# Sample rows: readouts gathered behind the fifth chunk step, new states computed beside the second feed-forward block

## The chip, the cores and the metric

The kernel runs on one core of a Trainium2 chip. A core has five engines with queues of their own: TensorE (PE, matmuls; its weight loads are shown as PEld), VectorE (DVE), ScalarE (ACT), GpSimd (POOL) and SyncE (SP, which here issues DMAs). Each works through its own queue in order, and an instruction whose input is not there holds all that stand behind it on that engine. The metric is the device time of one execution in microseconds (us); lower is better.

## The reference

One inference step of a small hybrid decoder: a half-step SwiGLU feed-forward block, a mixer, a second half-step feed-forward block and a final RMS norm. It works on one prompt of 512 tokens and on 8 sample rows, each a single new token with a stored state. The mixer has a pooling part and a state-space part with 16 heads of 64, in two groups, and a state of 128 per head and channel. For the prompt the state-space part is evaluated in chunks of 128 tokens. For a sample row it is one step of the recurrence:

```python
dt = softplus(dt_raw + dt_bias);  A = -exp(a_log)
h_new = exp(dt * A) * h0 + (dt * x) outer B      # 64 x 128 for each head
y     = h_new @ C  +  d_skip * x
y     = rms_norm_by_group(y * silu(z)) * ssd_norm
```

`y` goes on through the output projection, and `h_new` (8 rows, 16 heads, 64 x 128, 4 MB in float32) is an output itself. The feed-forward blocks compute `h + 0.5 * (silu(x @ wg) * (x @ wu)) @ wd` with 2816 hidden columns.

## The kernel before, in words

Tokens lie along the free dimension: 520 columns, 512 of the prompt and 8 samples, worked in two halves of 260. Every float32 product is made of three matmuls (`mm3`, lines 115 to 118) on a high and a low part; `split` (line 101) makes the parts of a weight tile with a cast on ACT (line 106) and a subtraction on DVE (line 107).

The feed-forward block (`Ffn`) goes through 22 tiles of 128 hidden columns. `step(f)` (line 329) runs one tile: seven products (`product`, line 264) on 7 combinations in place of 8, each evacuated by ACT (line 284); `gates` (silu on ACT, line 292) and `close` (cast of the hidden tile g on ACT, line 299, and its low part on DVE, line 300). `load` (line 245) fetches the tile's weights into one of two raw pairs by SP and splits them. After 8, 8 and 6 tiles, `down` (line 339), and for the last chunk `down_by_half`, multiplies the chunk by the down weights and adds it to `h`. The factor -0.5 times each token's norm factor is a tile `rn`, made once by `scales` (line 302) and applied at lines 356 and 408.

The mixer follows lists written by hand: CONV_PLAN, then GATE_PLAN, then LAST_PLAN. A letter and a number name a stage: `b`, `x` convolution tiles; `p`, `c`, `m` pooling; `A`, `B` the two halves of a chunk step (`ssd_a`, `ssd_b`; number j is chunk j % 4 of group j // 4); `z` gate projection; `sN` the next N sample items; `G`, `H` gate and norm of a group; `o`, `g`, `h` the output projection's three parts; `n` the first tile of the second feed-forward block. A sample item is a pair (row b, group g), 16 in all, group 0 first. The lists give the order in which instructions are traced; a scheduler, which simulates the program, then orders each engine's queue: traced earlier is preferred, but what is ready may pass. `keep_in_program_order` pins an instruction behind the one traced before it on its engine, and `issue_after` behind a named one; neither adds a wait for a result.

A sample item (`sample`, line 760) loads B and C of its row, broadcast to 128 partitions (`bcb`, line 764), and the state `h0` (256 KB, line 767) by SP; for each of four quarters ACT makes dt x B (line 771) and DVE the new state (line 772); SP stores the state (line 774); and DVE forms the readout, a product with C summed along the row (line 776). `gate` (line 877) multiplies with silu(z), and `gate_out` (line 888) squares, norms and splits for the output projection. The tiles `h0`, `bcb` and `ho` have two buffers each.

Of the kernel before, what the change touches and what calls it, by code (L numbers as in the profile page):

```python
# [9 lines left out]
F32 = mybir.dt.float32  # L10
# [6 lines left out]
P = 128  # L17
# [44 lines left out]
def tile_trunk_step(ctx: ExitStack, tc: tile.TileContext, ins: dict, outs: dict):  # L62
# [132 lines left out]
    class Ffn:  # L195
# [4 lines left out]
        def __init__(self, nx, i, wx, gp, direct):  # L200
            self.nx, self.i, self.wx, self.gp, self.direct = nx, i, wx, gp, direct
            self.w, self.A, self.BE, self.ac, self.g, self.tg, self.raw, self.banks, self.behind = ({} for _ in range(9))

# [98 lines left out]
        def scales(self):  # L302
            rstds(self.nx, f"f{self.i}")
            self.rn = self.wx.tile([P, NT], F32, tag="rn", bufs=1, name=f"rn{self.i}")
            nc.vector.tensor_scalar(out=self.rn, in0=self.nx[3], scalar1=-0.5, scalar2=None, op0=ALU.mult)

# [71 lines left out]
        def down_by_half(self, c, lo, after, wd):  # L378
# [26 lines left out]
            def done(d, b):  # L405
                hs = HALVES[b]
                t = self.wx.tile([P, 2, HB], F32, tag="tg", bufs=2, name=f"th{self.i}_{d}{b}")[:, 0]
                nc.vector.tensor_tensor(out=t, in0=banks[d, b][:, :HB], in1=self.rn[:, hs], op=ALU.mult)
                nc.vector.tensor_tensor(out=h[:, d, hs], in0=t, in1=h[:, d, hs], op=ALU.add)
                after(d, b, hs)  # L410
# [127 lines left out]
    f2["ffn"].rest(before2, after2)  # L538
    for p in (ps[0], g2, f2["hg"], f2["wx"]):
        p.release()  # L540


def mixer(tc, ins, outs, e):
    nc = tc.nc
    cst, act, wp, tmp, dr, pool = (e[x] for x in ("cst", "act", "wp", "tmp", "dr", "pool"))
    bank, load_unit, mm3, ws, v, rstd, rstds, vec, h, nx2, raw_tile, open_f2, fin, fill = (
        e[x] for x in ("bank", "load_unit", "mm3", "ws", "v", "rstd", "rstds", "vec", "h", "nx2", "raw_tile",
# [56 lines left out]
    rstds(nx2[0], "mx")  # L604
    dv = mp.tile([48, NT], F32, tag="h0", bufs=2, name="dv")
    for b, hs in enumerate(HALVES):
# [84 lines left out]
    def pooling(g):  # L691
# [15 lines left out]
        nc.gpsimd.tensor_tensor(out=cur[:, first], in0=cur[:, first], in1=rcnt[:, : w - 1], op=ALU.mult)  # L707
        held["pool"] = nc.gpsimd.tensor_tensor(out=cur[:, first], in0=cur[:, first], in1=U[:, first], op=ALU.subtract)
        nc.gpsimd.tensor_copy(npp[:, g], U[:, SEQ : SEQ + PAST])
# [22 lines left out]
    sdt = mp.tile([P, NX, NS], F32, tag="sdt", name="sdt")  # L732
    sdec = mp.tile([P, NX, NS], F32, tag="sdec", name="sdec")
    sxdt = mp.tile([P, NX, NS], F32, tag="sxdt", name="sxdt")
    ysm = mp.tile([P, NX, NS], F32, tag="ysm", name="ysm")
    scr_bc = dr.tile([NS, 512], F32, name="scr_bc")

    def sample_decay():
# [9 lines left out]
    def sample_bc():  # L748
        bcs = bank("bcs")
        for j in range(4):  # L750
            nc.tensor.transpose(bcs[:NS, j * P : (j + 1) * P], BC[:, j, SEQ:NT], ident)
        bct = mp.tile([NS, 512], F32, tag="ho", bufs=2, name="bct")
        nc.scalar.copy(bct, bcs[:NS, :])
        nc.sync.dma_start(out=scr_bc, in_=bct)

    def sample_x(g):
        gs = slice(4 * g, 4 * g + 4)
        nc.vector.tensor_tensor(out=sxdt[:, gs], in0=sdt[:, gs], in1=X[:, gs, SEQ:NT], op=ALU.mult)

    def sample(b, g):  # L760
        gs = slice(4 * g, 4 * g + 4)
        shp = [P, 4, P]
        bcb = mp.tile([P, 2, P], F32, tag="bcb", bufs=2, name=f"bcb{b}{g}")
        nc.sync.dma_start(out=bcb, in_=scr_bc.rearrange("b (a g n) -> b g a n", a=2, g=2)[b, g].unsqueeze(0)
                          .to_broadcast([P, 2, P]))
        h0 = mp.tile(shp, F32, tag="h0", bufs=2, name=f"h0_{b}{g}")
        nc.sync.dma_start(out=h0, in_=ins["state_ssm"][:, b, gs])
        o = mp.tile(shp, F32, tag="ho", bufs=2, name=f"ho_{b}{g}")
        for q in range(4):
            j = 4 * g + q  # L770
            nc.scalar.activation(out=o[:, q], in_=bcb[:, 0], func=AF.Copy, scale=sxdt[:, j, b : b + 1])
            nc.vector.scalar_tensor_tensor(out=h0[:, q], in0=h0[:, q], scalar=sdec[:, j, b : b + 1], in1=o[:, q],
                                           op0=ALU.mult, op1=ALU.add)
        nc.sync.dma_start(out=outs["nss"][:, b, gs], in_=h0)
        for q in range(4):
            nc.vector.scalar_tensor_tensor(out=o[:, q], in0=h0[:, q], scalar=1.0, in1=bcb[:, 1], op0=ALU.mult,
                                           op1=ALU.mult, accum_out=ysm[:, 4 * g + q, b : b + 1])

# [109 lines left out]
    def gate_out(g):  # L888
        zs = zbox[0]
        ry = mp.tile([P, NT], F32, tag="wph", name=f"yr{g}")  # L890
        acc = act.tile([P, NT], F32, tag="acc", name=f"yacc{g}")
        for b, hs in enumerate(HALVES):
            sq = [acc[:, hs]] + [tmp.tile([P, HB], F32, tag="ta", name=f"ysq{g}{q}{b}") for q in range(1, 4)]
            for q in range(4):
# [13 lines left out]
    def samples(n):  # L908
        for _ in range(n):
            if smp:  # L910
                with tc.issue_after(held["pool"].ins):
                    sample(*smp.pop(0))

# [133 lines left out]
```

## Time and profile before

| | us |
|---|---|
| median of 3 runs | 1028.15 |
| lowest, highest | 1027.37, 1032.51 |
| the profiled execution: time | 1030.91 |
| the profiled execution: span, first to last instruction | 1029.1 |

In the profile the first feed-forward block lies roughly between 0 and 370 us, the mixer up to 665 us, the second block from there to the end, with its last tile's output after 985 us. Busy time is the time in which an engine has at least one instruction running, taken from the trace; for PE, whose matmuls are pipelined, a stretch without gaps still says nothing of the rate, which the granted clock and the number of matmuls show. A row of a timeline gives start, length, engine, line, operation, output and inputs by the program's names, shape and count, and in brackets the idle time before it with what ended it. A row of waits reads "who waits, at which line, for whom", with the total, the number of times and the longest.

### The profile page before, as it was taken

Reading aid. Unit: us, or ns where it says so; the run is one execution under the profiler, and the core shown is the slowest. Engines: PE = TensorE matmul, PEld = TensorE weight load, DVE = VectorE, ACT = ScalarE, POOL = GpSimd, SP = SyncE. Lnnn points to the kernel's source line nnn. Section 1 sums busy time; section 2 is a strip of 40 time slices with the busy share of each in tenths; the row PEclk is TensorE's granted clock in tenths of the full one; section 3 lists DMA queues with packets and bytes.
Section 4 is the critical chain, followed back from the end, with each engine's and each line's share of the span. In section 5 each row is a group of like instructions: output and inputs, shape, how many; then the busy total and the mean of one; then the engine's idle time right before and its main releaser. Section 6 shows DMA issues by size and latency. Waiting matters only on the chain.

```text
span 1029.1 us, 19313 instructions
## 1 busy us (share of the span) xinstructions
PE 981.7 (95%) x7848; PEld 956.6 (93%) x7848; DVE 807.3 (78%) x1403; ACT 526.4 (51%) x884; POOL 57.0 (6%) x109
## 2 busy tenths in 40 slices
PE   7999999999999999997698999999999999999994
PEld 6999999999999999996598999899999999999994
DVE  7999557995578788689989877999954799557866
ACT  7566314663145555775486525656631566315552
POOL 0000000000000000337201000000000000000000
PEclk9999999999999999999899999999999999999997
DMA  5333223232232143355354222222323323232203
GB/s 186 111 124 123 83 87 119 83 124 82 88 118 93 55 138 116 126 173 183 110 174 145 94 103 82 69 96 91 115 83 103 103 88 119 82 103 104 93 32 83
DMA packets 45352, 110.25 MB, mean 107 GB/s; under 512 B 5896, under 2 KB 17096, under 8 KB 45264
## 3 DMA queue, kind: packets, MB, share of 16 engines
q1 hardware_dynamic: 45264, 109.03, 31.4%
q8 instruction: 61, 1.00, 0.4%
q14 instruction: 27, 0.22, 0.1%
HBM read 101.67 MB, written 7.34 MB: 106 GB/s over the span
## 4 chain that ended last, share of the span: by engine, by line
PE 42%; DVE 7%; ACT 4%; DMA 2%; issue 1%; POOL 1%; DVEq 0%; ACTq 0%; SPq 0%
PE A L116 4%; PE A L117 4%; PE A L118 4%; PE dn L118 3%; PE dn L116 3%; PE dn L117 3%; PE BE L116 3%; PE BE L118 3%; PE BE L117 3%; PE wo L116 2%; PE wo L118 2%; PE wo L117 2%; PE P L228 1%; PE dh L116 1%; DMA bcb<-scr_bc 1%
## 5 line engine op out<-in xcount | busy, mean ns | idle before, releaser
L356 DVE TENSOR_TENSOR td<-dn,rn 128x520 f32<-128x520 f32 x40 | 27.9, 699 | 112.5 <-PE dn L118 112.5
L116 PE MATMUL dn<-g,whi_1d 128*128 128x260 f32 x352 | 99.3, 283 | 1.7 <-ACT whi_1d L106 1.5
L117 PE MATMUL dn<-g,whi_1d 128*128 128x260 f32 x352 | 99.2, 282 | 0.0
L118 PE MATMUL dn<-g,wlo_1d 128*128 128x260 f32 x352 | 99.1, 283 | 0.0
L116 PE MATMUL dn<-g,whi_2d 128*128 128x260 f32 x256 | 72.5, 283 | 1.6 <-ACT whi_2d L106 1.6
L117 PE MATMUL dn<-g,whi_2d 128*128 128x260 f32 x256 | 72.3, 282 | 0.0
L118 PE MATMUL dn<-g,wlo_2d 128*128 128x260 f32 x256 | 72.1, 283 | 0.0
L116 PEld LDWEIGHTS dn<-g,whi_1d 128*128 128x128 f32 x352 | 66.1, 188 | 2.4 <-ACT whi_1d L106 2.0
L284 ACT COPY ac<-A 128x260 f32<-128x260 f32 x123 | 46.0, 375 | 41.3 <-PE A L118 39.7
L117 PEld LDWEIGHTS dn<-g,whi_1d 128*128 128x128 f32 x352 | 66.2, 188 | 0.0
L118 PEld LDWEIGHTS dn<-g,wlo_1d 128*128 128x128 f32 x352 | 66.1, 188 | 0.0
L106 ACT CAST whi_1d<-raw_1d 128x1024 fp32r<-128x1024 f32 (+1 forms) x24 | 23.4, 980 | 70.6 <-PE dn L117 62.2
L228 PE MATMUL P<-xg_f,raw 128*128 128x260 f32 x192 | 46.2, 398 | 5.3 <-DMA raw<-in_w1gu 5.2
L106 ACT CAST whi_2d<-raw_2d 128x1024 fp32r<-128x1024 f32 (+1 forms) x18 | 18.5, 1027 | 63.6 <-PE dn L117 59.2
L116 PEld LDWEIGHTS dn<-g,whi_2d 128*128 128x128 f32 x256 | 48.3, 189 | 2.0 <-ACT whi_2d L106 2.0
L256 DVE TENSOR_TENSOR s<-raw 128x1024 f32<-128x1024 f32 x41 | 49.9, 1217 | 0.0
L117 PEld LDWEIGHTS dn<-g,whi_2d 128*128 128x128 f32 x256 | 48.2, 188 | 0.0
L228 PEld LDWEIGHTS P<-xg_f,raw 128*128 128x128 f32 x192 | 37.5, 199 | 11.5 <-ACT xg_f L178 5.2
L118 PEld LDWEIGHTS dn<-g,wlo_2d 128*128 128x128 f32 x256 | 48.1, 188 | 0.0
L116 PE MATMUL wo<-catg,whi_wo 128*128 128x260 f32 x128 | 37.4, 292 | 0.2 <-DVE h L871 0.2
L116 PE MATMUL inz<-xh_mx,whi_inz 128*128 128x260 f32 x128 | 37.4, 292 | 0.0
L118 PE MATMUL inz<-xh_mx,wlo_inz 128*128 128x260 f32 x128 | 36.9, 288 | 0.0
(1334 smaller groups left out, 3920.3 us busy)
## 6 DMA issues: line engine op xcount, KB each, us to landing
raw<-in_w2gu SPq DMA_DIRECT2D x44, 512.0 KB, 3.7
raw<-in_w1gu SPq DMA_DIRECT2D x42, 512.0 KB, 4.4
raw_1d<-in_w1d SPq DMA_DIRECT2D x16, 512.0 KB, 3.7
raw_2d<-in_w2d SPq DMA_DIRECT2D x16, 512.0 KB, 4.4
raw_wo<-in_w_out SPq DMA_DIRECT2D x12, 512.0 KB, 4.6
h<-in_state_ssm SPq DMA_DIRECT2D x16, 256.0 KB, 4.8
ab<-scr_acs SPq DMA_DIRECT2D x8, 512.0 KB, 5.2
out_nss<-h SPq DMA_DIRECT2D x16, 256.0 KB, 3.3
```

The source lines that it names most:

```text
L106: nc.scalar.copy(h, src)
L116: nc.tensor.matmul(ps, whi, xhi, start=start, stop=False, **kw)
L117: nc.tensor.matmul(ps, whi, xlo, start=False, stop=False, **kw)
L118: nc.tensor.matmul(ps, wlo, xhi, start=False, stop=stop, **kw)
L228: nc.tensor.matmul(self.banks[f, u][b][:, :HB], ws(self.raw[f][:, u], j + 4 * q), xg[:, slot[q]], start=j == q == 0, stop=j == 3 and q == ...
L256: nc.vector.tensor_tensor(out=s1, in0=diag, in1=up0, op=ALU.add)
L284: nc.scalar.copy(keep, out[:, :HB])
L356: nc.vector.tensor_tensor(out=t, in0=banks[d][:, :, :HB], in1=self.rn.rearrange("p (b t) -> p b t", b=2), op=ALU.mult)
```

## The change

- **Readouts.** With C.h_new = exp(dt A) (C.h0) + (C.B) dt x, the readout no longer needs the new state. `sample` loads C alone (`cb`, in the tag `ta`, three buffers) and `h0` (now four buffers) and forms C.h0, four DVE operations for each item, each pinned. `sample_bc` adds the products C.B for all rows (one DVE operation, one matmul with ones, one ACT copy), and `sample_y`, three small DVE operations at the start of `gate`, puts the parts together.
- **New states.** A generator, `new_states`, called once in each `step(f)` of the second feed-forward block with f > 2: the first call loads B's row and `h0` of the first item; each of the next 16 loads the following item and processes one with eight ACT copies of 128 x 128 with a scale (dt x B, and exp(dt A) h0), an accumulating DMA that adds the one to the other in SBUF, and the store, both DMAs issued by POOL. Loads and copies are pinned. The states are so loaded twice.
- **Order.** GATE_PLAN has its first `s` after B4 and z3, group 0's eight items ahead of G0, which goes from before z4 to behind z5, and group 1's eight between B6 and G1, which goes from before o2 to behind it. `sample`'s `issue_after` goes.
- **Scale and squares.** `rn` goes; lines 356 and 408 multiply by -0.5 and by the norm in one operation. `gate_out` squares four full rows into X in place of eight half rows into `acc` and `ta`.

```diff
 GATE_PLAN = (
-    "s2 A4 z0 B3 z1 s2 m3 z2 s2 B4 z3 s2 A5 G0 z4 B5 A6 z5 s2 s2 z6 s2 A7 z7 B6 s2 o0 H0 o1 B7 G1 o2 "
+    "A4 z0 B3 z1 m3 z2 B4 z3 s2 A5 z4 s2 B5 A6 z5 s2 s2 G0 z6 A7 z7 B6 s2 o0 H0 s2 o1 B7 s2 o2 s2 G1 "
     "o3 g0 g1 H1 g2 g3"
 )
...
         def scales(self):
             rstds(self.nx, f"f{self.i}")
-            self.rn = self.wx.tile([P, NT], F32, tag="rn", bufs=1, name=f"rn{self.i}")
-            nc.vector.tensor_scalar(out=self.rn, in0=self.nx[3], scalar1=-0.5, scalar2=None, op0=ALU.mult)
...
         def step(self, f):
+            if self.states is not None and f > 2:
+                next(self.states, None)
...
-                nc.vector.tensor_tensor(out=t, in0=banks[d][:, :, :HB], in1=self.rn.rearrange("p (b t) -> p b t", b=2),
-                                        op=ALU.mult)
+                nc.vector.scalar_tensor_tensor(out=t, in0=banks[d][:, :, :HB], scalar=-0.5,
+                                               in1=self.nx[3].rearrange("p (b t) -> p b t", b=2), op0=ALU.mult,
+                                               op1=ALU.mult)
...
     g2 = f2["ffn"].gp = pool("g2", "left")
+    f2["st"] = pool("st2", "left")
+    f2["ffn"].states = f2["states"](f2["st"])
...
+        dots = bank("dots")[:, : 2 * NS]
+        nc.vector.tensor_tensor(out=sbc, in0=BC[:, 0:2, SEQ:NT], in1=BC[:, 2:4, SEQ:NT], op=ALU.mult)
+        nc.tensor.matmul(dots, ones, sbc.rearrange("p g b -> p (g b)"), start=True, stop=True)
+        nc.scalar.copy(sbc, dots.rearrange("p (g b) -> p g b", g=2))
...
     def sample(b, g):
+        cb = tmp.tile([P, HB], F32, tag="ta", name=f"cb{b}{g}")[:, :P]
+        nc.sync.dma_start(out=cb, in_=rows_bc(b, 1, g))
+        h0 = mp.tile([P, 4, P], F32, tag="h0", bufs=4, name=f"h0_{b}{g}")
+        nc.sync.dma_start(out=h0, in_=ins["state_ssm"][:, b, 4 * g : 4 * g + 4])
+        for q in range(4):
+            tc.keep_in_program_order(
+                nc.vector.scalar_tensor_tensor(out=junk, in0=h0[:, q], scalar=1.0, in1=cb, op0=ALU.mult, op1=ALU.mult,
+                                               accum_out=ysm[:, 4 * g + q, b : b + 1]))
+
+    def sample_y(g):
         gs = slice(4 * g, 4 * g + 4)
...
+        xb = mp.tile([P, 4, NS], F32, tag="xb", name=f"xb{g}")
+        nc.vector.tensor_tensor(out=xb, in0=sxdt[:, gs], in1=sbc[:, g : g + 1].to_broadcast([P, 4, NS]), op=ALU.mult)
+        nc.vector.tensor_tensor(out=ysm[:, gs], in0=ysm[:, gs], in1=sdec[:, gs], op=ALU.mult)
+        nc.vector.tensor_tensor(out=ysm[:, gs], in0=ysm[:, gs], in1=xb, op=ALU.add)
+
+    def new_states(wx):
+        def load(b, g):
+            br = wx.tile([P, P], F32, tag="sb", bufs=2, name=f"br{b}{g}")
+            tc.keep_in_program_order(nc.sync.dma_start(out=br, in_=rows_bc(b, 0, g)))
+            hs = wx.tile([P, 4, P], F32, tag="sh", bufs=2, name=f"hs{b}{g}")
+            tc.keep_in_program_order(nc.sync.dma_start(out=hs, in_=ins["state_ssm"][:, b, 4 * g : 4 * g + 4]))
+            return br, hs
+
+        todo = [(b, g) for g in range(2) for b in range(NS)]
+        ahead = load(*todo[0])
+        for i, (b, g) in enumerate(todo):
+            yield
+            br, hs = ahead
+            if i + 1 < len(todo):
+                ahead = load(*todo[i + 1])
+            o = wx.tile([P, 4, P], F32, tag="so", bufs=2, name=f"so{b}{g}")
+            for q in range(4):
+                j = 4 * g + q
+                for t, u, s in ((o, br, sxdt), (hs, hs[:, q], sdec)):
+                    tc.keep_in_program_order(
+                        nc.scalar.activation(out=t[:, q], in_=u, func=AF.Copy, scale=s[:, j, b : b + 1]))
+            nc.gpsimd.dma_start(out=hs, in_=o, accum_op=ALU.add)
+            nc.gpsimd.dma_start(out=outs["nss"][:, b, 4 * g : 4 * g + 4], in_=hs)
...
     def gate(g):
         zs = zbox[0]
         gs = slice(4 * g, 4 * g + 4)
+        sample_y(g)
...
-            sq = [acc[:, hs]] + [tmp.tile([P, HB], F32, tag="ta", name=f"ysq{g}{q}{b}") for q in range(1, 4)]
-            for q in range(4):
-                nc.scalar.activation(out=sq[q], in_=zs[:, 4 * g + q, hs], func=AF.Square)
-            rstd(ry, sq, hs, 512, f"y{g}{b}")
+            rstd(ry, [X[:, 4 * g + q, hs] for q in range(4)], hs, 512, f"y{g}{b}")
```

More of the change, by code (lines that the diff above doesn't have):

```diff
@@ L538, in tile_trunk_step @@
     f2["ffn"].rest(before2, after2)
-    for p in (ps[0], g2, f2["hg"], f2["wx"]):
+    for p in (ps[0], f2["st"], g2, f2["hg"], f2["wx"]):
         p.release()
@@ L732, in mixer, with rows_bc @@
     sdt = mp.tile([P, NX, NS], F32, tag="sdt", name="sdt")
-    sdec = mp.tile([P, NX, NS], F32, tag="sdec", name="sdec")
-    sxdt = mp.tile([P, NX, NS], F32, tag="sxdt", name="sxdt")
+    sdec = cst.tile([P, NX, NS], F32, tag="sdec", name="sdec")
+    sxdt = cst.tile([P, NX, NS], F32, tag="sxdt", name="sxdt")
     ysm = mp.tile([P, NX, NS], F32, tag="ysm", name="ysm")
+    sbc = mp.tile([P, 2, NS], F32, tag="sbc", name="sbc")
+    junk = act.tile([P, NT], F32, tag="acc", name="junk")[:, :P]
     scr_bc = dr.tile([NS, 512], F32, name="scr_bc")
+    def rows_bc(b, a, g):
+        return scr_bc.rearrange("b (a g n) -> b a g n", a=2, g=2)[b, a, g].unsqueeze(0).to_broadcast([P, P])
     def sample_decay():
@@ L769, in sample @@
-        for q in range(4):
[L770 to L777, printed above, removed]
+        cb = tmp.tile([P, HB], F32, tag="ta", name=f"cb{b}{g}")[:, :P]
@@ L910, in samples @@
             if smp:
-                with tc.issue_after(held["pool"].ins):
-                    sample(*smp.pop(0))
+                sample(*smp.pop(0))
     pooled, box = [], {}
```

23 lines of the change are left out of this document (10 added, 13 removed).

## The prediction

> **What bounds the kernel now.** I read the page's head, then the busy time by stage, then who TensorE (PE) waits for.
>
> ```profile
> span 1029.1 us, 19313 instructions
> PE 981.7 (95%) x7848; PEld 956.6 (93%) x7848; DVE 807.3 (78%) x1403; ACT 526.4 (51%) x884; POOL 57.0 (6%) x109
> ```
>
> PE is busy for 981.7 of 1029.1 us. Whatever removes work from another engine can return at most the 47.4 us in which PE idles, plus what slow clocks cost. The second view cuts the mixer's second half into stretches; its columns are the busy time (and instructions) of PE, weight loads, DVE, ACT and POOL, then the granted clock, the DMA share and GB/s.
>
> ```profile
> 440.00:500.00 60.00, 47.18 (x371) 42.01 (x369) 56.60 (x154) 36.01 (x87) 33.13 (x47) 0.94 0.49 158
> 500.00:560.00 60.00, 53.08 (x420) 49.82 (x421) 54.21 (x172) 40.89 (x88) 7.58 (x9) 0.94 0.46 148
> 560.00:575.00 15.00, 15.00 (x129) 14.07 (x128) 15.00 (x53) 9.37 (x17) 2.22 (x2) 1.00 0.44 149
> 575.00:632.00 57.00, 56.80 (x447) 54.61 (x446) 44.97 (x75) 21.76 (x34) 1.24 (x1) 1.00 0.24 84
> ```
>
> From 440 to 560 us PE idles 12.8 + 6.9 = 19.7 us while DVE is busy for 110.8 of 120 us. From 575 us on, in the output projection, PE is full again and DVE has 12.0 us to spare. The waits of PE between 400 and 640 us (total, times, longest) say on whom:
>
> ```profile
> PE yd L837 <- DVE ab L822: 7.7, 3, 3.5
> PE pst L834 <- DVE E L848: 6.8, 1, 6.8
> PE px L794 <- ACT X L673: 1.4, 1, 1.4
> PE pst L834 <- POOL xw L821: 1.2, 1, 1.2
> ```
>
> The two long ones, 14.5 us, end on DVE. Both belong to the chunk steps (ssd_a, ssd_b), whose DVE instructions stand in one queue with everything else. After the longest gap PE also runs slowly:
>
> ```profile
> 490.00:495.00 5.00, 1.18 (x2) 0.50 (x2) 5.00 (x11) 1.28 (x4) 1.68 (x5) 0.62 0.31 93
> 495.00:500.00 5.00, 3.82 (x23) 2.26 (x21) 5.00 (x15) 2.19 (x4) 1.29 (x2) 0.70 0.34 120
> 500.00:505.00 5.00, 4.33 (x23) 4.33 (x24) 5.00 (x20) 3.99 (x8) 0.35 (x2) 0.66 0.22 65
> ```
>
> PE's busy 1.18, 3.82 and 4.33 us at granted clocks of 0.62, 0.70 and 0.66 lose 0.4 + 1.1 + 1.5 = 3.0 us against a full clock. So 22.7 us can be won here and no more.
>
> **Mixer: what leaves DVE.** The sample rows' work on DVE is L772 (new state) and L776 (readout). Busy time of L772 in the first and the second 60 us, then the same for L776 (whose count includes one accumulator read for each readout):
>
> ```profile
> 440.00:500.00 60.00, 9.66 (x28) 0.94 0.49 158
> 500.00:560.00 60.00, 8.22 (x28) 0.94 0.46 148
> ```
>
> ```profile
> 440.00:500.00 60.00, 9.97 (x52) 0.94 0.49 158
> 500.00:560.00 60.00, 6.43 (x52) 0.94 0.46 148
> ```
>
> So each stretch holds 28 new-state operations and 26 readouts. What one holds the queue for I take from start to start, since successive instructions overlap:
>
> ```profile
> 447.20 1.66 DVE L772 SCALAR_TENSOR_TENSOR h<-h,sdec,ho 128x128 f32<-128x128 f32 x6
> ...
> 448.77 0.28 DVE L776 SCALAR_TENSOR_TENSOR ho<-h,bcb 128x128 f32<-128x128 f32 x1
> ...
> 448.98 0.29 DVE L776 SCALAR_TENSOR_TENSOR ho<-h,bcb 128x128 f32<-128x128 f32 x1
> ```
>
> Six of L772 in 1.66 us, counted as 1.57 us to the next row at 448.77, are 0.26 us each; a readout with its accumulator read is 0.21 us. The change takes all L772 out of the mixer and puts every readout behind the fifth chunk step. The first stretch loses 28 x 0.26 + 26 x 0.21 = 12.8 us of DVE time. The second loses the same 12.8 us and receives the eight rows of group 0, 32 readouts, 6.7 us, and four of the seven small new operations (the other three go to the later gate or to the earlier transposes), at most a readout's 0.21 us each, 0.8 us: a relief of 5.3 us. The rows of group 1 now stand between the output projection's units, another 32 x 0.21 = 6.7 us, and lie in the 12.0 us that DVE has free there; without that cover they would delay the gate of group 1 by 6.7 us at most. Together DVE is relieved by 18.1 us where PE waits for it.
>
> Not all of that reaches PE: about a quarter of PE's 19.7 us of waiting (19.7 - 14.5 = 5.2) ends on others or in short steps. I take three quarters of 18.1: **-13.6 us**. The ends are 0 (the chain of the chunk steps waits for something else next) and -22.7 us (all idle and all slow clock gone). What also leaves here and is priced at nothing: 64 ACT copies, 16 stores of 256 KB and the wait of the SP queue before each, since they only compete with the same steps and their gain is inside the same 22.7 us. The added matmul with ones and its copy, and the sums of squares done as four full rows in place of eight halves, lie under PE's 56.80 busy us of 57 or among those chunk steps.
>
> What the pin adds on DVE: a readout that waits for its broadcast row or its state (three and four buffers ahead) holds everything behind it, the chunk steps' ab, E and hst among it, and PE waits for those. Its bounds are 0 and the whole gain of the second stretch, 5.3 us.
>
> **Second feed-forward block: what arrives.** Sixteen steps (f = 4 to 19) each get eight ACT copies of 128x128, two loads on SP's queue and two DMAs on POOL's. The same form on ACT, eight in a row:
>
> ```profile
> 525.77 2.45 ACT L771 ACTIVATE ho<-bcb,sxdt 128x128 f32<-128x128 f32 x8
> ```
>
> A set costs 2.45 us. Two steps of the block, columns as before:
>
> ```profile
> 702.35:712.45 10.10, 10.10 (x87) 10.10 (x86) 9.97 (x14) 6.25 (x11) 0.00 (x0) 1.00 0.29 104
> 712.45:722.55 10.10, 10.10 (x87) 10.10 (x86) 9.37 (x13) 6.45 (x11) 0.00 (x0) 1.00 0.30 106
> ```
>
> PE has no gap in 10.10 us; ACT goes from 6.4 to 8.9 us, which fits. But DVE is busy for 9.4 to 10.0, so 0.1 to 0.7 us a step is all that it can lose. The copies are pinned behind the silu of the step before (L292). ACT and DVE there:
>
> ```profile
> 711.26 0.64 ACT L292 ACTIVATE tg<-tg 128x520 f32<-128x520 f32 x1
> 712.26 1.05 ACT L106 CAST whi_6a<-raw 128x1024 fp32r<-128x1024 f32 x1 [0.36 <-PE A L117]
> 713.31 0.63 ACT L299 CAST g<-tg 128x520 fp32r<-128x520 f32 x1
> 714.06 0.38 ACT L284 COPY ac<-A 128x260 f32<-128x260 f32 x1
> 715.13 1.06 ACT L106 CAST shi_6c<-s 128x1024 fp32r<-128x1024 f32 x1 [0.69 <-PE BE L117]
> ```
>
> ```profile
> 713.74 1.22 DVE L107 TENSOR_TENSOR wlo_6a<-raw,whi_6a 128x1024 fp32r<-128x1024 f32 x1
> 714.87 0.69 DVE L300 TENSOR_TENSOR g<-tg,g 128x520 fp32r<-128x520 f32 x1
> 716.22 1.23 DVE L107 TENSOR_TENSOR slo_6c<-s,shi_6c 128x1024 fp32r<-128x1024 f32 x1 [0.65 <-ACT shi_6c L106]
> ```
>
> If the eight run as one block from 711.9 to 714.35, the cast of g, the copy ac and the cast whi_6a queue behind it, and DVE, free at 713.74, waits about 1.2 us for g's cast (714.35 + 0.63) and again for whi_6a. Yet g is read only by the down product, and whi_6a by a product of the next step, so DVE can take other work of the block first, and ACT's own gaps (0.36, 0.69 and later ones) absorb the block within the step. The ends are 0 and 2.45 x 16 = 39 us; I take 0.15 us a step, near the lower end because both engines' sums stay under 10.10: **+2.4 us**.
>
> The transfers. Landing times (min, median, max) of the state load and of the state store in the mixer, and the weight loads on SP's queue in this block:
>
> ```profile
> DMA to landing us min/median/max: 3.3/4.8/7.4
> ```
>
> ```profile
> DMA to landing us min/median/max: 2.0/3.3/5.4
> ```
>
> ```profile
> 708.58 0.33 SPq L249 DMA_DIRECT2D raw<-in_w2gu  x1
> ...
> 718.68 0.33 SPq L249 DMA_DIRECT2D raw<-in_w2gu  x1
> ```
>
> With two buffers, a state's slot must pass copies, accumulating DMA, store and next load within two steps, 20.2 us: 2.45 + 3.3 + 4.8 = 10.6 leave 9.6 us for the accumulating DMA. The trace of before has none. Nearest rows: one load, 4.8 us, below; the slowest load and store in series, 12.8 us, above. I take 4.8, since it too is one transfer of 256 KB into SBUF. Then nothing waits. SP issues the weights of a step 10 us early (708.58 for a cast at 722), so a load pinned ahead of them may wait some 5 us unseen. POOL's queue is otherwise empty (0.00 us). The page "SBUF — State Buffer" of the Trainium skill (the "DVE blocks DMA" trap) speaks against this part: a DMA issued from POOL has its descriptors written by POOL's cores, which certain DVE instructions lock out. No run here shows such a DMA; the Trainium skill's "DMA: Bandwidth & Descriptors" (anatomy of one DMA) would give 2.0 us plus 0.6 us for 256 KB, an estimate by which the sum stays as it is.
>
> **The folded -0.5.** The operation at L305 goes, and the 56 multiplications after it gain a scalar:
>
> ```profile
> L305 DVE TENSOR_SCALAR rn<-r_f x2: 418/420/421, 29.7 to 671.4; 128x520 f32<-128x520 f32 x2
> ```
>
> ```profile
> L286 DVE TENSOR_TENSOR ac<-ac 128x260 f32<-128x260 f32 x41 | 17.2, 421 | 0.4 <-ACT ac L284 0.4
> ...
> L187 DVE SCALAR_TENSOR_TENSOR xd_f<-xd_f,xg_f 128x260 f32<-128x260 f32 x8 | 3.4, 420 | 0.0
> ```
>
> Two operands with or without a constant take the same, so 2 x 0.4 us go and nothing comes: **-0.8 us** at most; I take -0.8.
>
> **Sum.** -13.6 + 2.4 - 0.8 = -12.0 us. The profiled execution took 1030.91 us (span 1029.1), 2.8 above the median of the runs, 1028.15; from the first it gives 1018.9, from the median **1016**, which I forecast.
>
> **The rivals.**
> - *Everything in the mixer comes back*: all 22.7 us, 1028.15 - 22.7 - 0.8 + 2.4 = 1007. For it: DVE is full in the stretch with the gaps. Against: 5.2 us of the waits are not DVE's. Chance 0.10.
> - *Another wait takes the place*: the chunk steps' own order, or pinned readouts that wait for their rows, leave 5 us of the gain: 1028.15 - 5 - 0.8 + 2.4 = 1025. For it: ACT and POOL also end waits. Chance 0.14.
> - *Slower, in the feed-forward block*: ACT's block of copies holds the casts, DVE loses the 2.45 us less its spare 0.7, 1.75 us x 16 = 28 us: 1028.15 - 13.6 - 0.8 + 28 = 1042. It decides from 14.4 / 16 = 0.9 us a step. For it: DVE's 9.4 to 10.0 of 10.10. Against: what is delayed first is needed late. Chance 0.16.
> - *The accumulating DMA is slow*: at 12.8 us the slot's round is 23.4 us, 11.7 a step, 1.6 more x 13 steps (the first of each chunk has the down product to catch up) = 21 us: 1028.15 - 14.4 + 21 = 1035. Chance 0.08. The trap that the Trainium skill names would act here; nothing in the trace bears it out.
> - *It does not do what it says*, the copies fall elsewhere than into these steps: the pins leave ACT no other place, so it has no chance of its own.
>
> **Numbers.** The forecast has 0.52. Under 1023 (0.5%, about what can be told from no change) lie it, the first rival and 0.06 of the second: 0.68. Within 0.5% lie the rest of the second and 0.03 of the third, growing by little: 0.11. Slower: 0.21. The range from 1004 to 1036 leaves out the third rival's upper part; the likeliest case's own is 1010 to 1022.
>
> **What would show it.** L822 and L848 no longer end PE's waits near 470 and 490 us, and the clock stays at 1.00; about 28 readouts fewer before z3; in steps f = 4 to 19 PE stays at 10.10 us with ACT near 8.9. I am wrong if these steps grow, if copies wait on the state's load, or if PE's idle time from 440 to 560 us stays near 20 us.

## The result, and the profile after

The changed kernel takes 1020.51 us (median of 5 runs, 1018.54 to 1022.85), against 1028.15 before (the same median, now of 5 runs, 1027.37 to 1032.51). The ratio on record is 0.9909, with a 95% interval of 0.9895 to 0.9924: faster by 0.9%, or 9.4 us. The quotient of the two medians is 0.9926, a gain of 7.6 us, so the gain is 0.7 to 0.9%. The profiled execution took 1020.51 us, with a span of 1018.5 us at a mean granted clock of 0.991; before, the span was 1029.1. Those spans, which the traces below explain, differ by 10.6 us: the profiled execution of before lay 2.8 us above its median.

The head of the page of the changed kernel (busy time, share of the span, instructions):

```profile
span 1018.5 us, 19401 instructions
PE 978.0 (96%) x7850; PEld 954.2 (94%) x7850; DVE 791.7 (78%) x1344; ACT 539.5 (53%) x941; POOL 82.4 (8%) x141
```

PE does the same work (7850 matmuls against 7848). DVE lost 59 instructions and 15.6 us, ACT and POOL gained 13.1 and 25.4 us. The four stretches of the mixer, with the columns of the prediction:

```profile
440.00:500.00 60.00, 58.56 (x493) 54.30 (x492) 55.51 (x105) 40.99 (x82) 36.03 (x50) 1.00 0.31 106
500.00:560.00 60.00, 60.00 (x494) 56.75 (x494) 54.36 (x161) 30.97 (x49) 9.16 (x8) 1.00 0.44 145
560.00:575.00 15.00, 15.00 (x128) 14.07 (x128) 14.97 (x42) 3.96 (x6) 1.53 (x1) 1.00 0.22 74
575.00:632.00 57.00, 53.84 (x398) 51.36 (x397) 46.78 (x109) 24.59 (x33) 0.00 (x0) 1.00 0.24 84
```

From 440 to 560 us PE idles for 1.4 us (before: 19.7), its clock is 1.00, and it issues 987 matmuls where it issued 791. DVE is as busy as before, 109.9 us against 110.8, though with more of the mixer's work done in the same 120 us. In the last stretch, the output projection, PE now idles for 3.2 us (before: 0.2). PE's waits over the whole span (total, times, longest) name what is left:

```profile
PE A L116 <- ACT ac L285: 6.7, 8, 1.9
...
PE psr_y L160 <- ACT X L933: 1.6, 1, 1.6
...
PE A L118 <- DVE slo_8d L107: 1.5, 1, 1.5
...
PE wo L117 <- DVE catg L942: 1.3, 2, 0.6
```

The waits for ab and E are gone. New are two in the output projection, for the gate of group 1 (psr_y, catg), one in the second block, for the low part of a weight tile (slo_8d), and one of 1.3 us in the tail. The waits for evacuations (ac) grew; before, they were

```profile
PE A L116 <- ACT ac L284: 2.7, 6, 1.4
```

To see where the time went, I cut each profiled execution at four instructions: the last matmul of the second block's norm (psr_f), the first and last matmul of its down products before the last chunk (dn), and the first operation of the last chunk's output (th). Those rows of the changed kernel (duration min/median/max, then first and last start):

```profile
L160 PE MATMUL psr_f<-acc_f,ones x8: 382/382/383, 24.0 to 645.5; 128*128 128x260 f32 x8
L116 PE MATMUL dn<-g,whi_2d x256: 277/283/386, 733.2 to 916.0; 128*128 128x260 f32 x128
L410 DVE SCALAR_TENSOR_TENSOR th<-dh,r_f x16: 419/426/429, 973.5 to 999.8; 128x260 f32<-128x260 f32 x16
```

The table has such cuts for every kernel of this study, from its one profiled execution (us; each column but the first is a difference of two cuts, the last one up to the span's end):

| kernel | mixer's end | to first dn | to last dn | to first th | to the end |
|---|---|---|---|---|---|
| before | 666.2 | 86.7 | 179.0 | 55.0 | 42.2 |
| after | 645.5 | 87.7 | 182.8 | 57.5 | 45.0 |
| e1_rl_own | 645.7 | 88.0 | 183.0 | 59.0 | 42.3 |
| e2_fold_alone | 667.6 | 85.9 | 178.9 | 55.1 | 46.4 |
| e3_no_states | 645.9 | 86.0 | 178.9 | 55.0 | 46.3 |
| e4_sh3 | 646.2 | 85.9 | 182.9 | 57.5 | 46.4 |
| e5_old_plan | 641.3 | 87.1 | 183.4 | 57.5 | 46.6 |
| e6_down | 645.4 | 86.0 | 185.4 | 55.1 | 45.9 |
| e7_down_rl | 645.7 | 85.9 | 185.8 | 55.0 | 42.2 |
| b1_no_l772 | 661.0 | 86.7 | 179.0 | 55.0 | 41.7 |
| b2_no_l771 | 670.4 | 86.8 | 179.0 | 55.0 | 42.6 |
| b3_no_store | 662.5 | 86.7 | 179.0 | 55.0 | 41.9 |
| b4_no_part | 662.6 | 86.7 | 179.0 | 55.0 | 41.8 |
| e8_best | 641.8 | 87.7 | 178.9 | 55.4 | 42.0 |

So the change won 20.7 us in the mixer and gave back 1.0 + 3.8 + 2.5 + 2.8 = 10.1 us behind it.

### The profile page after: what moved, and what is told of

It is laid out like the page before. It is cut to its first block, busy times and chain, and to the rows that moved or that the text cites. A ratio compares the mean times of both kernels' runs of the same rounds, so it can differ in the third digit from the quotient of the medians.

```text
span 1018.5 us, 19401 instructions
## 1 busy us (share of the span) xinstructions
PE 978.0 (96%) x7850; PEld 954.2 (94%) x7850; DVE 791.7 (78%) x1344; ACT 539.5 (53%) x941; POOL 82.4 (8%) x141
## 4 chain that ended last, share of the span: by engine, by line
PE 83%; DVE 7%; ACT 6%; issue 2%; POOL 1%; DMA 0%; SPq 0%; DVEq 0%; ACTq 0%
PE A L116 7%; PE A L117 7%; PE dn L116 7%; PE dn L118 7%; PE A L118 7%; PE dn L117 7%; PE BE L116 6%; PE BE L117 6%; PE BE L118 6%; PE P L229 2%; PE wo L116 2%; PE wo L117 2%; PE wo L118 2%; PE inz L116 2%; PE inz L118 2%
## 5 line engine op out<-in xcount | busy, mean ns | idle before, releaser
L357 DVE SCALAR_TENSOR_TENSOR td<-dn,r_f 128x520 f32<-128x520 f32 x40 | 27.9, 700 | 112.7 <-PE dn L118 112.7
L229 PEld LDWEIGHTS P<-xg_f,raw 128*128 128x128 f32 x192 | 37.3, 198 | 11.5 <-ACT xg_f L178 5.2
L117 PE MATMUL wo<-catg,whi_wo 128*128 128x260 f32 x128 | 36.4, 285 | 1.3 <-DVE catg L942 1.3
L116 PE MATMUL wo<-catg,whi_wo 128*128 128x260 f32 x128 | 37.3, 293 | 0.3 <-DVE h L911 0.3
L814 POOL DMA_DIRECT2D hs<-so x16 | 13.9, 868 | 286.7 <-ACT hs L813 146.3
```

Source lines behind the costliest of these rows:

```text
L116: nc.tensor.matmul(ps, whi, xhi, start=start, stop=False, **kw)
L117: nc.tensor.matmul(ps, whi, xlo, start=False, stop=False, **kw)
L229: nc.tensor.matmul(self.banks[f, u][b][:, :HB], ws(self.raw[f][:, u], j + 4 * q), xg[:, slot[q]], start=j == q == 0, stop=j == 3 and q == ...
L357: nc.vector.scalar_tensor_tensor(out=t, in0=banks[d][:, :, :HB], scalar=-0.5, in1=self.nx[3].rearrange("p (b t) -> p b t", b=2), op0=ALU.mult,
L814: nc.gpsimd.dma_start(out=hs, in_=o, accum_op=ALU.add)
```

## The experiments

Every kernel ran in five rounds beside the kernel before, whose median in these sessions was 1031.15 to 1032.03 us; so ratios to it are compared, and 0.001 is about 1.03 us. The changed kernel itself ran only in its own session; a difference to it carries the intervals of both ratios, 1.4 to 2.2 us each way.

**The tail.** The fold of -0.5 keeps the norm factor r_f in use up to the last th. The tile r_last of the final norm has the same slot (tag "r"), so the first half's final norm, which could start early, must wait. The reciprocals on r_last before and after:

```profile
L532 DVE RECIPROCAL r_last<-r_last x4: 955/960/967, 1003.5 to 1021.7; 128x130 f32<-128x130 f32 x4
```

```profile
L537 DVE RECIPROCAL r_last<-r_last x4: 907/958/967, 1003.0 to 1009.3; 128x130 f32<-128x130 f32 x4
```

Before, the first one starts 11.9 us ahead of the last th (1015.4); after, 3.2 us behind it (999.8). Experiment e1_rl_own gives r_last a slot of its own in the changed kernel:

```diff
-    rl = act.tile([P, NT], F32, tag="r", name="r_last")
+    rl = f2["st"].tile([P, NT], F32, tag="rl", name="r_last")
```

> The changed kernel with one edit: the final norm's tile r_last gets a place of its own instead of the slot of r_f, which the folded -0.5 keeps in use until the last down product. Theory: the first half's final norm waits for the last reader of r_f, which costs the tail 2.8 us; here its first reciprocal runs about 1002 - 13 = 989 us after the start, under the second half's matmuls, and the time falls from 1020.5 to about 1017.7 us. Rival (the order in the tail has another cause): the tail stays as it is, 1020.5 us.

Measured: 1019.53 us, above the 1017.7 that I expected; ratio 0.9881 (0.9867 to 0.9895), by the ratios 2.9 us better than after, with intervals that just touch. The reciprocals start early again, 11.8 us ahead of the last th (1004.1):

```profile
L537 DVE RECIPROCAL r_last<-r_last x4: 957/962/968, 992.3 to 1009.9; 128x130 f32<-128x130 f32 x4
```

Experiment e2_fold_alone puts only the fold into the kernel before:

```diff
-            self.rn = self.wx.tile([P, NT], F32, tag="rn", bufs=1, name=f"rn{self.i}")
-            nc.vector.tensor_scalar(out=self.rn, in0=self.nx[3], scalar1=-0.5, scalar2=None, op0=ALU.mult)
...
-                nc.vector.tensor_tensor(out=t, in0=banks[d, b][:, :HB], in1=self.rn[:, hs], op=ALU.mult)
+                nc.vector.scalar_tensor_tensor(out=t, in0=banks[d, b][:, :HB], scalar=-0.5, in1=self.nx[3][:, hs],
+                                               op0=ALU.mult, op1=ALU.mult)
```

> The kernel before with the folded -0.5 alone (rn goes). Theory: DVE gains 0.8 us at two places that hide it, and r_last waits for r_f's last reader: the tail grows by about 2.8 us, 1030 to 1031 us. Rival, the prediction's own term: -0.8 us, 1027.4 us.

Measured: 1034.86 us, ratio 1.0033 (1.0022 to 1.0045): 3.4 us slower. The last column grows from 42.2 to 46.4, and the other columns move by 1.4 us at most. That the shared slot is what costs this is shown by the runs that give r_last its own: the last column falls by 2.7 us in e1_rl_own and by 3.7 in e7_down_rl below. In e1_rl_own the column before it grew by 1.5 us, and the spans of the two kernels differ by 0.5 us only. In that execution PE's clock was 0.83 just after a place where two sets of copies meet (see below), which on its 9.26 busy us costs 1.6 us:

```profile
936.00:946.00 10.00, 9.26 (x64) 9.27 (x65) 6.91 (x9) 5.94 (x12) 1.43 (x2) 0.83 0.45 143
```

**What the new states cost in the second block.** Experiment e3_no_states is the changed kernel without them (their output stays unwritten):

```diff
-    f2["ffn"].states = f2["states"](f2["st"])
```

> The changed kernel without its new states: their loads, copies, accumulating DMAs and stores are left out, and the output of new states is not written. Theory: of the 10.2 us that the second feed-forward block grew by, 7.4 us are the states' work and 2.8 us the tail, so 1020.5 - 7.4 = 1013.1 us, with steps of 10.10 us and no wait of PE for ac beyond those of before. Rival (the block starts worse because of the mixer's end): at least 1017 us.

Measured: 1014.27 us, ratio 0.9835 (0.9821 to 0.9848), 7.6 us better than after by the ratios and 6.4 by the spans. The table's middle columns return to before's 179 and 55, and the mixer's end (645.9) does not move. Where the states cost is in the trace of the changed kernel. Behind a down product two steps' silus follow each other by 5.1 us, and the pinned copies of each stand right behind (ACT's timeline, the first and the last copy of each set and what follows; start, length):

```profile
794.99 0.63 ACT L293 ACTIVATE tg<-tg 128x520 f32<-128x520 f32 x1
795.53 0.39 ACT L813 ACTIVATE so<-br,sxdt 128x128 f32<-128x128 f32 x1
...
797.58 0.39 ACT L813 ACTIVATE hs<-hs,sdec 128x128 f32<-128x128 f32 x1
...
800.13 0.64 ACT L293 ACTIVATE tg<-tg 128x520 f32<-128x520 f32 x1
800.67 0.39 ACT L813 ACTIVATE so<-br,sxdt 128x128 f32<-128x128 f32 x1
...
802.72 0.39 ACT L813 ACTIVATE hs<-hs,sdec 128x128 f32<-128x128 f32 x1
803.01 0.36 ACT L285 COPY ac<-A 128x260 f32<-128x260 f32 x1
```

PE waits 1.95 us for that copy ac at 803.01. The windows there, an undisturbed step, and the second such place:

```profile
706.20:716.30 10.10, 10.10 (x86) 10.10 (x85) 10.05 (x15) 8.36 (x18) 1.42 (x2) 1.00 0.56 132
```

```profile
796.00:806.00 10.00, 8.05 (x61) 7.73 (x60) 9.32 (x16) 9.49 (x25) 2.28 (x3) 0.93 0.63 176
806.00:816.00 10.00, 10.00 (x78) 10.00 (x77) 7.31 (x11) 6.28 (x15) 0.57 (x1) 0.90 0.59 186
...
926.00:936.00 10.00, 8.09 (x66) 7.77 (x64) 9.19 (x16) 9.34 (x25) 1.42 (x2) 1.00 0.38 102
```

One set a step fits: PE full, ACT at 8.36 of 10.10 us. Two sets in 10 us do not: ACT is at 9.4, PE loses 2 us, and at the first place the clock falls to 0.93 and 0.90 as well.

**The queue of SP.** The state load of a set waits for its slot, and the weights of a coming step are issued right behind it; DVE then waits for them:

```profile
712.58 0.33 SPq L798 DMA_DIRECT2D hs<-in_state_ssm  x1
713.01 0.37 SPq L250 DMA_DIRECT2D raw<-in_w2gu  x1
```

```profile
720.07 1.23 DVE L257 TENSOR_TENSOR s<-raw 128x1024 f32<-128x1024 f32 x1 [2.67 <-DMA raw<-in_w2gu]
```

The slot comes free through the store on POOL, which itself waits for the accumulating DMA (POOL's timeline):

```profile
703.21 0.86 POOL L814 DMA_DIRECT2D hs<-so  x1 [4.11 <-ACT hs L813]
709.76 0.57 POOL L815 DMA_DIRECT2D out_nss<-hs  x1 [5.69 <-DMA hs<-so]
```

```profile
hs<-so POOLq DMA_DIRECT2D x16, 256.0 KB, 4.3
```

The last row, of the DMA groups, gives count, size and median landing time. Here, from the issue of the accumulation to the store, 6.55 us pass, and 2.82 us more until the load is issued. From one step to the next the weights' issue at L250 slips in this chunk: 689.86, 701.36 and 713.01 us, 11.5 and 11.7 us apart, where a step takes 10.10. Experiment e4_sh3 gives the state a third buffer:

```diff
-            hs = wx.tile([P, 4, P], F32, tag="sh", bufs=2, name=f"hs{b}{g}")
+            hs = wx.tile([P, 4, P], F32, tag="sh", bufs=3, name=f"hs{b}{g}")
```

> The changed kernel with three buffers for the state tile hs instead of two. Theory: SP's queue no longer waits for the store of the item two before, so the weights of a step are again issued about 10 us early and PE's wait of 1.5 us for slo_8d at 717 us goes; the two waits of 1.9 us behind double sets of copies stay: 1018 to 1019.5 us. Rival (ACT's blocks alone cost the time): 1020.5 us, and the wait near 717 us stays.

Measured: 1020.64 us, ratio 0.9902 (0.9888 to 0.9917), not to be told from after; I had expected 1018 to 1019.5. In the trace the first chunk gets its 1.8 us back (87.7 to 85.9, less than before's 86.7) and PE's wait for slo_8d is gone; the columns up to the first th stay, and the last one is 1.4 us longer. So the wait was real and small.

**The sets elsewhere.** Experiment e6_down moves the sets from the steps into the sixteen units of the two down products, where I took ACT to be freer (with three state buffers):

```diff
-            if self.states is not None and f > 2:
+            if self.states is not None and f == 3:
                 next(self.states, None)
...
+                if self.states is not None and after is None:
+                    next(self.states, None)
```

> The changed kernel with the 16 sets of new states moved from the steps to the 16 units of the first two down products, where ACT is busy for some 2 of 10 us and DVE for 4, and three buffers for hs. Theory (a set costs time only where ACT and DVE have none to spare): the block loses the 7.4 us, the tail's 2.8 us stay, 1013 to 1014 us. Rival (it is the transfers that cost: SP's queue is held by state loads, the down weights come late): 1018 us or more, with PE waiting for whi_2d.

Measured: 1020.25 us, ratio 0.9895 (0.9874 to 0.9916). My expectation fell: the loss moved with the sets and did not shrink. The column up to the last dn is 185.4, 6.4 us above before, because in a down product the casts of its weights come just in time, and now stand behind a set (not, as the rival had it, because transfers came late):

```profile
PE dn L118 <- DVE wlo_2d L107: 7.3, 8, 1.3
```

Experiment e7_down_rl adds the slot of its own for r_last to that kernel (the edit of e1_rl_own).

> As the run with the sets at the down products, and r_last in a place of its own. Theory: both losses go, 1010 to 1011 us, 17 to 18 us below the kernel before. Rival: what the one saves the other takes back in the tail, 1013 us or more.

Measured: 1016.39 us, ratio 0.9854 (0.9832 to 0.9875), 4.2 us better than e6_down by the ratios, the tail's cost once more; the time is the rival's, since the sets' cost stayed.

**The order in the mixer.** Experiment e5_old_plan gives the changed kernel the GATE_PLAN of before; everything else, the pins too, stays:

```diff
-    "A4 z0 B3 z1 m3 z2 B4 z3 s2 A5 z4 s2 B5 A6 z5 s2 s2 G0 z6 A7 z7 B6 s2 o0 H0 s2 o1 B7 s2 o2 s2 G1 "
+    "s2 A4 z0 B3 z1 s2 m3 z2 s2 B4 z3 s2 A5 G0 z4 B5 A6 z5 s2 s2 z6 s2 A7 z7 B6 s2 o0 H0 o1 B7 G1 o2 "
```

> The changed kernel with the hand-written order GATE_PLAN of before: 6 of the 16 readout items stand again ahead of the fifth chunk step, and the gates of both groups are where they were. The new states stay in the second feed-forward block. Theory (where the readouts stand matters): 24 readouts of 0.21 us, 5.0 us of DVE time, return to the stretch in which DVE is full, PE idles there again, and the time rises by 3 to 5 us to about 1024 us. Rival (taking the new states, their ACT copies and their stores out is what freed the mixer): within 1 us of 1020.5 us.

Measured: 1018.04 us, ratio 0.9869 (0.9849 to 0.9890): not slower, as I had expected, but faster than after. The mixer ends at 641.3 in place of 645.5. PE no longer waits in the output projection and issues 431 matmuls there in place of 398:

```profile
575.00:632.00 57.00, 57.00 (x431) 55.37 (x430) 46.66 (x80) 26.54 (x36) 0.00 (x0) 1.00 0.25 87
```

So the new places in the plan are no gain. By the traces the loss of 4.2 us comes with group 1: the first psr_y starts alike in both kernels (551.6 and 551.8), the last one, group 1's, at 594.5 in after and at 590.4 here, and the waits that are gone are psr_y's and catg's. The new plan puts both group 1's readouts (the last at 585.3 in after, 572.8 here) and its gate G1 later; no run moves one of them alone. Between the chunk steps the old plan does no harm, because the pins hold the readouts back under it as well (below).

**The parts of the old work alone.** What in the mixer brings the 20.7 us? Three kernels each take one part out of the kernel before: the new-state operation on DVE (b1_no_l772: the state goes out as loaded), the ACT copies (b2_no_l771: DVE adds B itself, without its factor), the stores (b3_no_store: the output stays unwritten).

```diff
 # b1_no_l772
-            nc.vector.scalar_tensor_tensor(out=h0[:, q], in0=h0[:, q], scalar=sdec[:, j, b : b + 1], in1=o[:, q],
-                                           op0=ALU.mult, op1=ALU.add)
 # b2_no_l771
-            nc.scalar.activation(out=o[:, q], in_=bcb[:, 0], func=AF.Copy, scale=sxdt[:, j, b : b + 1])
-            nc.vector.scalar_tensor_tensor(out=h0[:, q], in0=h0[:, q], scalar=sdec[:, j, b : b + 1], in1=o[:, q],
+            nc.vector.scalar_tensor_tensor(out=h0[:, q], in0=h0[:, q], scalar=sdec[:, j, b : b + 1], in1=bcb[:, 0],
 # b3_no_store
-        nc.sync.dma_start(out=outs["nss"][:, b, gs], in_=h0)
```

> The kernel before without its 64 DVE operations of L772: the state as loaded is stored and read out, so new states and the sample rows' readouts are not the reference's. ACT's copies, the loads and the stores stay. Theory (DVE bounds the mixer's second half): 64 x 0.26 = 17 us leave DVE and the time falls by 9 to 13 us. Rival (ACT's copies or the SP queue held the chunk steps): at most 4 us.

> The kernel before without its 64 ACT copies of L771: L772 adds B itself in place of dt x B, so new states and the sample rows' readouts are not the reference's. Theory (DVE bounds): ACT loses 19 us of work and 17 us of waits for B's rows in its queue, the time falls by 0 to 4 us. Rival (ACT's queue held the chunk steps): 8 us or more.

> The kernel before without the 16 stores of the new states at L774, whose output is left unwritten. Theory (DVE bounds): the SP queue no longer waits for L772 ahead of weights and decay rows, 0 to 3 us. Rival (SP's queue held the chunk steps): 8 us or more.

Measured: 1025.51 us, ratio 0.9942 (0.9925 to 0.9959), for b1_no_l772; 1035.48 us, 1.0033 (1.0018 to 1.0047), for b2_no_l771; 1028.52 us, 0.9971 (0.9958 to 0.9984), for b3_no_store. That is 6.0 us gained, 3.4 us lost and 3.0 us gained. Neither theory's number for the DVE operation held (9 to 13 us, or 4 at most), and to take ACT's copies away makes the kernel slower. The stores fit their theory (0 to 3 us). The three sum to 5.6 us. Experiment b4_no_part takes all three out together:

```diff
-            nc.scalar.activation(out=o[:, q], in_=bcb[:, 0], func=AF.Copy, scale=sxdt[:, j, b : b + 1])
-            nc.vector.scalar_tensor_tensor(out=h0[:, q], in0=h0[:, q], scalar=sdec[:, j, b : b + 1], in1=o[:, q],
-                                           op0=ALU.mult, op1=ALU.add)
-        nc.sync.dma_start(out=outs["nss"][:, b, gs], in_=h0)
```

> The kernel before without the sample rows' new states altogether: the ACT copies (L771), the new-state operation on DVE (L772) and the store (L774) are left out, so the output of the new states stays unwritten and the readouts, which stay at their old places in the old plan, read the state as it was loaded. Alone, the DVE operation was worth 6.0 us, the stores 3.0, and leaving out the copies cost 3.4. Theory (the three together hold the item loop back: each buffer of the state passes load, copies, operation, store; only with all gone does the mixer get its time back): ratio to before near 0.980, the last matmul of the convolution-to-output part (psr_f) at 641 to 647 us, a gain of 19 us or more. Rival (the parts add up, and the rest of the mixer's 20.8 us comes from the pinned readouts, the deeper buffers and the lighter loads): ratio 0.988 to 0.995, psr_f at 654 to 660 us.

Measured: 1026.82 us, ratio 0.9957 (0.9942 to 0.9971): 4.4 us. The theory fell, and by more than the rival had said: with no new state left in the mixer, it ends at 662.6 us, 3.6 earlier than before, no earlier than without the stores alone (662.5), while e5_old_plan, with the same plan, ends it at 641.3. The other 21.3 us are not the work that left.

The traces show what differs. Busy time (and count, with the accumulator reads) of the readouts alone in stretches of 15 us, first in b4_no_part, then in e5_old_plan:

```profile
440.00:455.00 15.00, 5.71 (x32) 1.00 0.43 125
455.00:470.00 15.00, 3.78 (x32) 1.00 0.68 215
470.00:485.00 15.00, 4.60 (x32) 0.89 0.50 164
485.00:500.00 15.00, 4.83 (x16) 0.74 0.66 201
```

```profile
440.00:455.00 15.00, 0.00 (x0) 1.00 0.44 137
455.00:470.00 15.00, 0.00 (x0) 1.00 0.22 72
470.00:485.00 15.00, 0.00 (x0) 1.00 0.37 125
485.00:500.00 15.00, 0.87 (x6) 1.00 0.25 82
```

Without pins, 112 of the 128 instructions run before 500 us; with pins 6. What that does, in DVE's timeline of b4_no_part:

```profile
489.86 1.15 DVE L772 SCALAR_TENSOR_TENSOR ho<-h,bcb 128x128 f32<-128x128 f32 x1
...
491.15 1.61 DVE L772 SCALAR_TENSOR_TENSOR ho<-h,bcb 128x128 f32<-128x128 f32 x1
...
492.91 1.12 DVE L772 SCALAR_TENSOR_TENSOR ho<-h,bcb 128x128 f32<-128x128 f32 x1
...
494.39 0.30 DVE L772 SCALAR_TENSOR_TENSOR ho<-h,bcb 128x128 f32<-128x128 f32 x1
494.61 0.68 DVE L844 TENSOR_TENSOR E<-yd,E 128x512 f32<-128x512 f32 x1
```

and in PE's:

```profile
495.44 2.05 PE L830 MATMUL pst<-xw,bt 128*128 128x512 f32 x2 [4.29 <-DVE E L844]
```

Eight readouts stand from 489.86 to 494.61 ahead of the chunk step's E, and PE waits 4.29 us for E. Five of them take the usual 0.28 us; the three shown take 3.0 us more than that together, beside work of POOL (the last section). So of this wait the place in the queue is one part, and the meeting with POOL the larger. (In the rows of the changed kernel above POOL is busy for 36.0 us from 440 to 500, and for 9.2 us from 500 to 560.) In the kernel before it is the same: ahead of the E for which PE waits 6.8 us, two readouts and a new-state operation take 1.34, 1.12 and 1.61 us.

The E above is the first of the mixer's six. PE's matmuls for it (yd) start at 477.53, so that it comes 17.1 us behind them. In e5_old_plan they start at 471.73, E (L888 there) follows 3.6 us behind, and the second E too runs before the first readout:

```profile
475.30 0.68 DVE L888 TENSOR_TENSOR E<-yd,E 128x512 f32<-128x512 f32 x1
...
487.85 0.68 DVE L888 TENSOR_TENSOR E<-yd,E 128x512 f32<-128x512 f32 x1
...
490.78 0.28 DVE L783 SCALAR_TENSOR_TENSOR junk<-h,cb 128x128 f32<-128x128 f32 x1
```

For b2_no_l771 the trace shows that PE's wait for ab grows from 7.7 to 10.9 us; that the new states, with no copies to wait for, come still earlier into DVE's queue is a reading and not shown. What stays open: the pins alone, put on the kernel before, were not run. The two kernels compared also differ in the state's buffers (four against two), in the row loaded (C alone against B and C) and in the gate's squares. So that the order makes the 21.3 us is read from the traces and not shown by a run of its own.

**All together.** Experiment e8_best is the changed kernel with the GATE_PLAN of before, r_last in its own slot, three state buffers, the first load ahead of the steps, and the sets in steps that don't follow a down product:

```diff
+STATE_STEPS = (2, 3, 4, 5, 6, 7, 8, 9, 12, 13, 14, 15, 16, 17, 20, 21)
...
-            if self.states is not None and f > 2:
+            if self.states is not None and f in STATE_STEPS:
...
+    next(f2["ffn"].states)
```

> The changed kernel with four edits: GATE_PLAN of before, r_last in a place of its own, three buffers for hs, and the 16 sets at steps 2 to 9, 12 to 17, 20 and 21, leaving out the two steps after each down product in which ACT catches up. Theory: the order gives 4 us, the tail 4 us, the double sets and the held weights 5 to 7 us: about 1007 to 1010 us where the kernel before takes 1031. Rival (sets cost wherever they stand among the steps): 1012 us or more.

Measured: 1007.92 us (1007.77 to 1009.03), ratio 0.9767 (0.9749 to 0.9785): 24.0 us below before by the ratio, within the 1007 to 1010 us expected, and by the ratios 14.6 us below the change as made. The table's columns return to before's but for 1.0 us in the first chunk and 0.4 in the third, with the sixteen sets in the block. At the place where two sets met, and now none runs, PE and clock are full:

```profile
796.00:806.00 10.00, 10.00 (x85) 10.00 (x85) 10.00 (x15) 7.45 (x14) 0.00 (x0) 1.00 0.32 109
```

## Why the prediction was right, and where its steps were not

The direction and roughly the size were right (1016 forecast, 1020.51 measured, inside the range of 1004 to 1036), but the terms erred in both directions: by the spans the mixer gave 7.1 us more (20.7 for 13.6), the rest cost 8.5 us more (10.1 for 1.6). That the sum came out so near is luck. Of its own signs, the idle time of PE from 440 to 560 us fell to 1.4 us and the clock stayed at 1.00, as forecast, and no copy waited for its state's load; but some steps of the block grew, which it had named as a sign of being wrong.

- **The mixer's term**: the step that failed is "together DVE is relieved by 18.1 us where PE waits for it", of which three quarters were to reach PE. Work did leave DVE, 15.6 us over the whole span, but PE did not gain three quarters of it: the work taken out was worth 6.0 us for the DVE operation alone and 4.4 for the whole part. By the traces what brought the time was the order: with the readouts behind the chunk steps' operations and out of POOL's busy stretch, PE's waits for ab and E went. I had priced the pin only as a cost (0 to 5.3 us), never as the gain.
- **The bound of 22.7 us** was too low: e5_old_plan gained 24.9. The idle 19.7 us were counted, but the slow matmuls only where the clock stood at 0.62 to 0.70, 3.0 us. By counts, after's 987 matmuls in 118.56 busy us are 0.120 us each, and before's 791 took 100.26 us in place of 95.0: 5.3 us of slow work, and 19.7 + 5.3 = 25.0. (An estimate, since the shapes are mixed.)
- **Where the readouts stand**: the plan's new places were credited with relieving the first stretch. The pins do that under the old plan too. And group 1's readouts, hidden by DVE's 12.0 spare us in the output projection by the prediction, together with G1's new place made group 1's gate late: 4.2 us, within the 6.7 named as the price without cover. DVE did have the time; by the traces what counted was when G1, and with it the output projection's last input, came.
- **The pinned readouts holding DVE**: not seen; PE is idle for 1.4 us in all from 440 to 560 us.
- **ACT's copies in the block**: the form was right (a set takes 2.4 us as one block, with eight starts 0.29 us apart; one set a step hides, with ACT at 8.36 for the forecast 8.9), and the size wrong: 6.4 to 7.6 us for 2.4, of which some 1.8 are the queue of SP (next point). The sixteen steps are not alike: behind each of the two down products two sets fall within about 5 us. I looked at two even steps and multiplied by sixteen.
- **Accumulating DMA and SP**: 4.8 us were assumed; it landed in 4.3 in the median, and the 12.8 us of the rival were not reached by any. Yet the slot's round did exceed the two steps, as that rival had said (11.5 and 11.7 us a step beside its 11.7), though 9.6 us of slack had been worked out: the sum left out that the store on POOL comes only 6.55 us behind the accumulation's issue and the load 2.82 us behind that, and that the chain also starts late (the accumulation waits for ACT). The price was not the rival's 21 us but 1.5 us of PE, once: the weights' lead absorbed the rest, as the prediction had argued, until DVE waited 2.67 us for them.
- **The fold**: -0.8 predicted, +3.4 measured alone. Operation times were right; what the sum lacked was the lifetime of r_f, whose slot r_last needs.
- **Squares and matmul with ones**: not run alone. With them in the kernel, e5_old_plan's output projection is full (57.00 of 57.00 us), so a cost there is not to be seen.

## What to carry to other kernels

On an engine that is full but not the bound, ask in what order its queue runs before adding up what leaves it: filler work that may run as soon as its data is there can stand ahead of the few operations the bounding engine waits for, and taking other work out then need not help. Look also at what the other engines do where the filler runs. Put added filler into every step only after looking at the steps that differ, those behind a change of phase. When an operation is folded away, look at which tile lives longer for it and whose slot that is.

## What the runs showed of the hardware

Readouts on DVE usually take 0.28 us, but a few take far longer beside POOL's work. In b4_no_part (min/median/max):

```profile
L772 DVE SCALAR_TENSOR_TENSOR ho<-h,bcb x64: 275/280/1614, 442.2 to 508.6; 128x128 f32<-128x128 f32 x64
```

The three slow ones shown above, ending at 491.01, 492.76 and 494.03, lie beside two sums of the pooling and a product of the chunk step:

```profile
489.59 3.02 POOL L703 TENSOR_TENSOR PW<-PW 128x648 f32<-128x648 f32 x2
...
492.78 1.09 POOL L839 TENSOR_TENSOR hst<-hst,cd 128x512 f32<-128x512 f32 x1
```

The first sum ends at 490.86, the second at 492.61, the product at 493.87: each readout ends about 0.15 us behind one of them. The Trainium skill gives a reason on its page "SBUF — State Buffer" (SBUF: two separate sides): DVE instructions with two inputs in SBUF and POOL instructions that read SBUF exclude each other for a whole instruction. The trace agrees. In b4_no_part six of the 64 readouts are stretched so, by 5.8 us together, all before 500 us. In e5_old_plan it is five, by 3.6 us, all behind 500 us, and there PE is busy for 60.00 of the 60 us up to 560: the same meeting costs nothing where PE does not wait.

The prediction also weighed that page's "DVE blocks DMA" trap (Trainium skill), by which certain DVE instructions hold up DMAs issued from POOL. All of DVE's rows in the block are TENSOR_TENSOR and SCALAR_TENSOR_TENSOR, and for these it was not to be seen: with DVE busy for 9 to 10 of 10 us POOL took 0.87 us to issue the accumulating DMA, in the mean of 16 (0.85 to 1.04). Whether other DVE instructions would hold it up, no run here shows.

```profile
L814 POOL DMA_DIRECT2D hs<-so x16 | 13.9, 868 | 286.7 <-ACT hs L813 146.3 <-DVE s L259 119.5 <-ACT ac L285 21.0
```

To land, these accumulations took from 3.3 to 7.5 us; what spreads them is open.
